# Program order for GpSimd and the SP queue in the first MLP product of a streaming encoder step

## The chip, the cores and the metric

The kernel runs on one core of one Trainium2 chip. The metric is the device time of one execution in microseconds (us); the times given are medians of several runs. The engines are named as the profile names them: PE is TensorE (PEld its weight loads), DVE is VectorE, ACT is ScalarE, POOL is GpSimd, and SP is SyncE, which here only issues DMAs. SP's queue works in order: while one DMA waits for its semaphore, those behind it wait too.

## The reference, cut to what matters

The reference is one inference step of a two-layer encoder over 1024 prompt tokens and 64 sample tokens, in fp32. Each layer ends with an MLP, the part that the change touches:

```
x = x + sq_relu_mlp(rmsnorm(x, norm_mlp[layer]), w_up[layer], w_down[layer])
def sq_relu_mlp(h, w_up, w_down):
    return jnp.square(jax.nn.relu(h @ w_up)) @ w_down
```

D_MODEL is 1024, D_FF 4096. The rest (pooling mixer and RG-LRU in layer 0, windowed attention in layer 1, cross-attention in both, norms, state outputs) is the same in both kernels.

## The kernel before, in words

Activations are kept transposed, features on the 128 partitions, tokens along the free axis. The 1088 tokens are cut into s = 0 (512 tokens) and s = 1 (576 tokens, worked on as two blocks of 288). Every fp32 product is made of three fp32r products of high and low parts, so each weight tile is loaded (`st`, line 174, three buffers), and split by ACT and DVE into `wp` (lines 186 and 187, three buffers). Class `Weights` does that along one plan of all weights: `ahead()` (line 192) splits up to two tiles beyond the one in use and loads as many further tiles as there are staging buffers.

The second product of the MLP, `mlp_down`, is one Strassen-like step with seven products (`SEVEN`). It needs sums of quarters of u (the squared activations) and sums of quarters of w_down. Both are made by POOL during the first product, `mlp_up` (line 934), and go through DRAM: u into `us`, the sums of weights into `sums`.

`mlp_up` loops over 16 turns q of two blocks f of 128 features. A turn works on one tile `u` (two buffers). For each f and each of three token blocks, `unit` multiplies (line 216, 24 matmuls), evacuates with the factor `rb` of the norm (DVE, line 969, into `t`, two buffers) and squares into u (ACT, lines 972 and 974). After both f, POOL makes four differences of u (line 990), and u is queued to be stored. Then `weights_sums(q)` loads quarters of w_down by two DMAs into the single buffer `quarters` (line 943) and POOL makes four sums (lines 947 to 950), queued to be stored too. `store()` (line 955) empties that one list, `todo`, after f = 0 of the next turn. In q = 0 and q = 15 the order of the blocks differs, so that s = 0 is used first; in q = 15, after s = 0's last block, four loads `load_u` (line 928) into `ur` (three buffers) and their splits `uhl` (lines 233 and 236) prepare the second product. `uhl` lies in the pool `hp`, whose eight buffers the two norms' pairs `hpH` and `hpL` fill until then.

`rb` comes from `Norm.columns` and `Norm.rows`: sums of squares `ss` (DVE, line 300), PE (line 310), `rc` (DVE, line 315), a power on POOL (line 316), transposes on PE (line 326), a copy on ACT (line 327). For s = 1 this is `prepared(1, G_MLP + l)`, called in line 1456 right before `mlp_up`.

What sets the order: the program states the instructions in an order, and a scheduler of the framework chooses the order of each engine's queue from it, by dependencies, priority and a simulation of its own. It may take `weights_sums` of later turns, which depend on nothing but their buffer, ahead of differences of u. A region `manual_schedule(engines=...)` makes the named engines issue the region's instructions in the stated order; other engines, and where instructions from outside the region fall among those inside, stay the scheduler's.

Of the kernel before, what the change touches and what calls it, by code (L numbers as in the profile page):

```python
# [24 lines left out]
G_MIX, G_CROSS, G_MEM, G_MLP, G_FIN = 0, 2, 4, 6, 8  # L25
# [21 lines left out]
def body(ctx, tc, I, O):  # L47
# [24 lines left out]
    def mm_bank():  # L72
        return bank(ps_mm, "mm")

    def s_bank():
        return bank(ps_s, "s")
# [54 lines left out]
    sums = [[scr.tile([128, 4, 2, 512], F32, name=f"sums{l}_{g}") for g in range(8)] for l in range(2)]  # L131
# [802 lines left out]
    def mlp_up(l, norms, p, outer):  # L934
        blocks = [(0, 0, 512), (1, 0, 288), (1, 288, 288)]
        us = [scr.tile([128, 7, 2, TH], F32, name=f"u{l}_{g}") for g in range(8)]
        todo, first = [], []

        def weights_sums(q):

            a = p.tile([128, 4, 512], F32, tag="quarters", name="quarters", bufs=1)
            for i in range(2):
                nc.sync.dma_start(a[:, 2 * i:2 * i + 2],
                                  I["w_down"][l][256 * q + 128 * i:256 * q + 128 * i + 128]
                                  .rearrange("p (h n) -> p h n", h=2))

            pool.tensor_tensor(a[:, 3], a[:, 1], a[:, 3], OP.add)
            pool.tensor_tensor(a[:, 1], a[:, 0], a[:, 1], OP.subtract)
            pool.tensor_tensor(a[:, 0], a[:, 3], a[:, 0], OP.subtract)
            pool.tensor_tensor(a[:, 2], a[:, 2], a[:, 0], OP.subtract)  # L950
            todo.append((sums[l][q // 2][:, :, q % 2], a))

        def store():
            while todo:
                nc.sync.dma_start(*todo.pop(0))

        for q in range(16):
            u = p.tile([128, 8, TH], F32, tag="u", name="u", bufs=2)
            wts = {}

            def unit(f, bi):
                s, b0, bn = blocks[bi]
                nm = norms[s]
                ps = s_bank() if q == 0 and s else mm_bank()
                dense(ps[:, :bn], wts[f], 0, KC, nm.pair.rhs(b0, bn))
                if q == 0 and f == 0 and b0 == 0:
                    nm.rows()
                t = p.tile([128, 512], F32, tag="t", name="t", bufs=2)
                dve.scalar_tensor_tensor(t[:, :bn], ps[:, :bn], 0.0, nm.rb[:, b0:b0 + bn], OP.max, OP.mult)  # L969
                slots = u[:, U21:U22 + 1] if f else u[:, U11:U12 + 1:U12 - U11]  # L970
                if s == 0:
                    act.activation(slots[:, :, :256], t.rearrange("p (a b) -> p a b", a=2), AF.Square)  # L972
                else:
                    act.activation(slots[:, b0 // 288, 256:], t[:, :bn], AF.Square)  # L974

            order = [[(f, bi) for bi in range(3)] for f in range(2)]
            if q in (0, 15):
                order = [[(0, 0)], [(1, 0), (0, 1), (0, 2), (1, 1), (1, 2)]]
            for f in range(2):
                wts[f] = W.get((("up", l), 2 * q + f))  # L980
                for o in order[f]:
                    unit(*o)
                    if q == 15 and o == (1, 0):
                        store()
                        first = [load_u(us, outer, 0, g) for g in range(4)]
                W.ahead()
                if f == 0:
                    store()
            for to, a, b in ((T1, U12, U11), (T3, U22, U12), (T2, U22, T1), (T4, T2, U21)):
                pool.tensor_tensor(u[:, to], u[:, a], u[:, b], OP.subtract)  # L990
            todo.append((us[q // 2][:, :, q % 2], u[:, :7]))
            weights_sums(q)
        store()
        return us, first

    def mlp_down(l, us, first, last, p, outer):
# [55 lines left out]
    class Window:  # L1052
# [124 lines left out]
        def store(self, ps, nm):  # L1177
            p = self.p
            nat = p.tile([128, 256], F32, tag="nat", name="nat", bufs=1)
            act.activation(nat, ps[:, :256], AF.Copy)  # L1180
            pool.dma_start(O[nm + "_p"][0, 0].rearrange("m k d -> m (k d)"), nat)
            nat = p.tile([128, 256], F32, tag="nat", name="nat", bufs=1)
            act.activation(nat[:64], ps[:64, 256:512], AF.Copy)
            pool.dma_start(O[nm + "_s"][0, 0, 64:128].rearrange("m k d -> m (k d)"), nat[:64])
# [182 lines left out]
    def prepared(s, g):  # L1367
        norm = Norm(s, g)
        for c in range(KC):
            norm.chunk(c)  # L1370
        norm.rows()
        return norm

    def phase(name):
        return tc.tile_pool(name=name, bufs=1, reuse_waits="tile")
# [24 lines left out]
    def main():  # L1400
        with phase("memory") as p:
            mem = memory_load(p)
            kv = memory_kv(p, *mem)
            next(kv)
            load_vectors(p)
            todo = [load_x(s) for s in range(2)]
            for _ in kv:
                for _ in range(5):
                    if todo and next(todo[0], "end") == "end":
                        todo.pop(0)  # L1410
            assert not todo
        norm = prepared(0, G_MIX)
        with phase("mixer") as p:
            q = Queue()
            mx = Mixer(p, q)
            first = mx.project(0, norm)
            for _ in IN_ORDER[1:]:
                next(first)
                q.step(5)
            next(first)  # L1420
            norm = prepared(1, G_MIX)
            q.step(5)
            second = mx.project(1, norm)
            for _ in range(3):
                next(second)
                q.step(5)
            while any(not job.done for job in mx.jobs[0]):
                q.step()
            project_back(0, ("out", 0), mx.y[0], q)
            mx.open[1] = True  # L1430
            for _ in second:
                q.step(5)
            c1 = prepared(0, G_CROSS)
            q.drain()
            project_back(1, ("out", 1), mx.y[1], order=[(0, 1, 2, 4, 5, 6), (7,), (3,)], spare=2)
            mx.states()
        for l in range(2):
            if l == 1:
                with phase("window") as p:
                    win = Window(p)  # L1440
                    win.caches()
                    win.project(0, norms[0])
                    win.attend()
                    norm = prepared(1, G_MIX + 1)
                    project_back(0, ("wo", 0), win.o, order=HALVES, spare=4)
                    win.project(1, norm)
                    win.attend()
                    c1 = prepared(0, G_CROSS + 1)
                    project_back(1, ("wo", 1), win.o, order=HALVES, spare=2)
            with phase(f"cross{l}") as p:  # L1450
                nexts = []
                cross(l, 0, c1, p, lambda: nexts.append(prepared(1, G_CROSS + l)))
                cross(l, 1, nexts[0], p, lambda: nexts.append(prepared(0, G_MLP + l)))
            with phase(f"mlp{l}") as outer:
                with phase(f"up{l}") as p:
                    up = mlp_up(l, [nexts[1], prepared(1, G_MLP + l)], p, outer)
                norms = [None, None]

                def last(s):
                    if s > l:  # L1460
                        while True:
                            yield
                    norms[s] = Norm(s, G_FIN, pair=False) if l else Norm(s, G_MIX + 1)
                    for c in range(4, 8):
                        norms[s].chunk(c)
                    for c in range(4):
                        yield
                        norms[s].chunk(c)
                    if l:
                        store_y(norms[s], s_bank)  # L1470
                    else:
                        norms[s].rows(s_bank)

                with phase(f"down{l}") as p:
                    mlp_down(l, *up, last, p, outer)

    main()


# [28 lines left out]
```

## Time and profile before

| | |
|---|---|
| Median of 3 runs | 2814.31 us (2809.4 to 2815.35) |
| Profiled execution, its own time | 2806.5 us |
| Its span, first to last instruction | 2804.7 us |
| Mean granted TensorE clock | 0.985 |
| Busy: PE, DVE, ACT, POOL | 2720.7, 1414.6, 1094.2, 535.8 us |

The span is what the instructions of the profiled execution cover; its own time is 1.8 us longer, and the median of the runs is 7.8 us above that execution. In the rows below times are us from the span's start. The first product of layer 0 begins at about 670 us and ends at about 1075 us; that of layer 1 lies at about 2040 to 2442 us. "x8" at a row's end counts merged instructions; "[9.93 <-POOL rc L316]" says that the engine sat idle for 9.93 us before it and what ended that.

### The profile page before, as it was taken

The page shows a single profiled execution, that of the slowest core. Times are in us where ns is not written, and L with a number is a line of the kernel's source. Part 1 is how long each engine was busy: PE and PEld are TensorE (multiplying, and loading weights), DVE is VectorE, ACT ScalarE, POOL GpSimd, SP SyncE. Part 2 cuts the span into 40 slices and gives each one's busy share as a digit, 9 for nine tenths or more (in the row PEclk, how much of TensorE's full clock was granted, in tenths as well). Part 3 has the DMA queues.
Part 4 walks back from the last instruction along what each step waited for, and adds up shares of the span by engine and source line. Part 5 has one row for each costly group of instructions (what it writes and reads, how often), then busy time and mean ns, then how long its engine had stood idle before and what let it go on. Part 6 is the DMA issues. An engine that isn't in the chain of part 4 may idle for free. (4 is left out here: it accounts for less than half of the span.)

```text
span 2804.7 us, 44507 instructions
## 1 busy us (share of the span) xinstructions
PE 2720.7 (97%) x18280; PEld 2540.8 (91%) x18280; DVE 1414.6 (50%) x2328; ACT 1094.2 (39%) x1929; POOL 535.8 (19%) x486
## 2 busy tenths in 40 slices
PE   8999999998998999999999999999989999999998
PEld 7978998897998999999988899989979989899998
DVE  5596766564322226455457558566532222464453
ACT  5584555352212124333337347344422112343334
POOL 3200000013455321000003013001245442300000
PEclk9999999999999999999999999999989999999999
DMA  8722232325666537555421321233366763465552
GB/s 269 226 83 75 68 102 81 106 84 173 221 224 222 181 129 242 186 186 178 132 66 31 86 71 38 88 92 99 113 203 209 253 232 127 142 238 182 176 179 79
DMA packets 364367, 411.89 MB, mean 147 GB/s; under 512 B 45840, under 2 KB 267040, under 8 KB 364164
## 3 DMA queue, kind: packets, MB, share of 16 engines
q1 hardware_dynamic: 355268, 382.00, 42.0%
q0 software_dynamic: 8896, 27.06, 2.9%
q8 instruction: 143, 2.34, 0.3%
q14 instruction: 60, 0.49, 0.1%
HBM read 299.74 MB, written 109.39 MB: 146 GB/s over the span
## 5 line engine op out<-in xcount | busy, mean ns | idle before, releaser
L216 PE MATMUL mm<-hpH,wp 128*128 128x288 f32 (+2 forms) x5952 | 1428.3, 329 | 16.9 <-DVE t L969 13.1
L216 PEld LDWEIGHTS mm<-hpH,wp 128*128 128x128 f32 x5952 | 1018.8, 189 | 98.4 <-DVE t L969 15.2
L216 PE MATMUL mm<-hpL,wp 128*128 128x288 f32 (+2 forms) x2976 | 932.9, 330 | 2.2 <-DVE hpL L291 2.2
L216 PEld LDWEIGHTS mm<-hpL,wp 128*128 128x128 f32 x2976 | 565.2, 190 | 42.0 <-DVE hpL L291 3.3
L186 ACT ACTIVATE wp<-st 128x1024 fp32r<-128x1024 f32 x282 | 297.8, 1058 | 672.3 <-PE mm L216 414.2
L187 DVE TENSOR_TENSOR wp<-st,wp 128x1024 fp32r<-128x1024 f32 x282 | 357.0, 1267 | 277.2 <-ACT wp L186 274.8
L969 DVE SCALAR_TENSOR_TENSOR t<-mm,rb 128x288 f32<-128x288 f32 (+1 forms) x184 | 99.1, 539 | 521.4 <-PE mm L216 458.0
L990 POOL TENSOR_TENSOR u<-u 128x544 f32<-128x544 f32 x128 | 203.8, 1606 | 233.3 <-ACT u L974 230.8
L316 POOL TENSOR_TENSOR rc<-rc,mhalf 128x4 f32<-128x4 f32 (+1 forms) x21 | 21.5, 1030 | 888.1 <-DVE rc L315 888.1
L972 ACT ACTIVATE u<-t 128x512 f32<-128x512 f32 x64 | 40.4, 632 | 371.2 <-DVE t L969 216.6
L1039 PE MATMUL s<-uhl,wd 128*128 128x256 f32 x560 | 156.5, 280 | 0.0
L1038 PE MATMUL s<-uhl,wd 128*128 128x256 f32 x560 | 156.1, 279 | 0.0
L1040 PE MATMUL s<-uhl,wd 128*128 128x256 f32 x560 | 156.0, 279 | 0.0
L236 DVE TENSOR_TENSOR uhl<-ur,uhl 128x1088 fp32r<-128x1088 f32 x112 | 146.2, 1307 | 16.5 <-ACT uhl L233 16.4
L186 ACT ACTIVATE wd<-st 128x1024 fp32r<-128x1024 f32 x70 | 73.9, 1056 | 199.5 <-PE t L1040 157.0
L216 PE MATMUL s<-hpH,wp 128*128 128x288 f32 (+1 forms) x576 | 141.4, 330 | 0.0
L233 ACT ACTIVATE uhl<-ur 128x1088 fp32r<-128x1088 f32 x112 | 123.1, 1103 | 36.6 <-DMA ur<-u 32.4
L216 PEld LDWEIGHTS s<-hpH,wp 128*128 128x128 f32 x576 | 98.1, 188 | 8.0 <-ACT hpH L233 0.3
L1038 PEld LDWEIGHTS s<-uhl,wd 128*128 128x128 f32 x560 | 105.3, 188 | 0.0
L1039 PEld LDWEIGHTS s<-uhl,wd 128*128 128x128 f32 x560 | 105.1, 188 | 0.0
L1040 PEld LDWEIGHTS s<-uhl,wd 128*128 128x128 f32 x560 | 105.0, 187 | 0.0
L187 DVE TENSOR_TENSOR wd<-st,wd 128x1024 fp32r<-128x1024 f32 x70 | 87.8, 1254 | 32.4 <-ACT wd L186 32.2
(367 smaller groups left out, 4798.7 us busy)
## 6 DMA issues: line engine op xcount, KB each, us to landing
u<-u SPq DMA_DIRECT2D x32, 1904.0 KB, 8.4
ur<-u SPq DMA_DIRECT2D x112, 544.0 KB, 5.7
quarters<-in_w_down_dram SPq DMA_DIRECT2D x64, 512.0 KB, 5.2
sums<-quarters SPq DMA_DIRECT2D x32, 1024.0 KB, 5.4
st<-in_w_up_dram SPq DMA_DIRECT2D x64, 512.0 KB, 6.6
st<-sums SPq DMA_DIRECT2D x64, 512.0 KB, 5.5
st<-in_w_down_dram SPq DMA_DIRECT2D x48, 512.0 KB, 4.7
st<-in_w_mq_dram SPq DMA_DIRECT2D x32, 512.0 KB, 3.6
```

Source lines behind the costliest of these rows:

```text
L186: act.activation(wt[:, 0], st, AF.Copy)
L187: dve.tensor_tensor(wt[:, 1], st, f32(wt[:, 0]), OP.subtract)
L216: pe.matmul(ps, a, b, start=i == 0, stop=i == len(terms) - 1)
L233: act.activation(h, src, AF.Copy)
L236: dve.tensor_tensor(l, src, f32(h), OP.subtract)
L316: pool.tensor_tensor(rc[:m, b0:b1], rc[:m, b0:b1], mhalf[:m, b0:b1], OP.pow)
L969: dve.scalar_tensor_tensor(t[:, :bn], ps[:, :bn], 0.0, nm.rb[:, b0:b0 + bn], OP.max, OP.mult)
L972: act.activation(slots[:, :, :256], t.rearrange("p (a b) -> p a b", a=2), AF.Square)
L990: pool.tensor_tensor(u[:, to], u[:, a], u[:, b], OP.subtract)
L1038: pe.matmul(ps, wl, uh, start=first, stop=False)
L1039: pe.matmul(ps, wh, ul, start=False, stop=False)
L1040: pe.matmul(ps, wh, uh, start=False, stop=half == 1 and g == 3 and k == 1)
```

## The change

The list of stores is split in two, `todo` for sums of u and `kept` for sums of weights. After f = 0 of a turn only the store of u is issued; the weights' store is issued after f = 1, just before the turn's own differences of u are stated. Everything in `mlp_up` that runs on SP and POOL is put into a region in which these two engines keep the stated order. `prepared(1, ...)` is called ahead of that region.

```diff
-        todo, first = [], []
+        todo, kept, first = [], [], []
...
-            todo.append((sums[l][q // 2][:, :, q % 2], a))
-
-        def store():
+            kept.append((sums[l][q // 2][:, :, q % 2], a))
+
+        def store(todo):
             while todo:
                 nc.sync.dma_start(*todo.pop(0))
...
                 for o in order[f]:
                     unit(*o)
                     if q == 15 and o == (1, 0):
-                        store()
+                        store(todo)
+                        store(kept)
                         first = [load_u(us, outer, 0, g) for g in range(4)]
                 W.ahead()
                 if f == 0:
-                    store()
+                    store(todo)
+            store(kept)
             for to, a, b in ((T1, U12, U11), (T3, U22, U12), (T2, U22, T1), (T4, T2, U21)):
                 pool.tensor_tensor(u[:, to], u[:, a], u[:, b], OP.subtract)
             todo.append((us[q // 2][:, :, q % 2], u[:, :7]))
             weights_sums(q)
-        store()
+        store(todo)
+        store(kept)
         return us, first
...
-                    up = mlp_up(l, [nexts[1], prepared(1, G_MLP + l)], p, outer)
+                    own = [nexts[1], prepared(1, G_MLP + l)]
+                    with tc.manual_schedule(engines={mybir.EngineType.SP, mybir.EngineType.Pool}):
+                        up = mlp_up(l, own, p, outer)
```

## Rows read from the trace of the kernel before

**Rows 1.** Waits of PE, whole span: total us, times, longest us.

```profile
PE t L326 <- POOL rc L316: 21.8, 6, 9.9
PE mm L216 <- DVE t L969: 13.1, 5, 4.5
...
PE t L310 <- DVE ss L300: 4.7, 2, 2.7
PE s L1038 <- DVE wp L187: 4.4, 2, 2.2
```

**Rows 2.** Busy time by stretch: busy us (count) of each engine, PEclk, DMA share, GB/s.

```profile
667.00:690.00 23.00, 10.34 (x56) 8.34 (x54) 11.74 (x14) 7.39 (x11) 11.52 (x10) 0.78 0.46 139
...
940.00:963.60 23.60, 23.60 (x147) 21.71 (x146) 5.67 (x8) 4.93 (x8) 6.81 (x5) 1.00 0.38 128
```

**Rows 3.** Waits of ACT from 700 to 930 us: total, times, longest.

```profile
ACT u L972 <- DMA u<-u: 79.8, 6, 19.1
```

**Rows 4.** Groups from 714 to 927 us: busy, mean ns, idle before, releaser.

```profile
L990 POOL TENSOR_TENSOR u<-u 128x544 f32<-128x544 f32 x36 | 52.7, 1481 | 5.8 <-ACT u L974 5.1
...
L947 POOL TENSOR_TENSOR quarters<-quarters 128x512 f32<-128x512 f32 x11 | 16.2, 1472 | 98.8 <-DMA quarters<-in_w_down_dram 98.8
```

**Rows 5.** Timeline of DVE, the 512-column evacuations: start us, us, instruction.

```profile
714.71 0.69 DVE L969 SCALAR_TENSOR_TENSOR t<-mm,rb 128x512 f32<-128x512 f32 x1 [3.14 <-PE mm L216]
...
927.32 0.69 DVE L969 SCALAR_TENSOR_TENSOR t<-mm,rb 128x512 f32<-128x512 f32 x1 [1.81 <-PE mm L216]
...
1033.58 0.69 DVE L969 SCALAR_TENSOR_TENSOR t<-mm,rb 128x512 f32<-128x512 f32 x1 [3.08 <-PE mm L216]
...
2085.81 0.69 DVE L969 SCALAR_TENSOR_TENSOR t<-mm,rb 128x512 f32<-128x512 f32 x1 [3.14 <-PE mm L216]
...
2294.68 0.69 DVE L969 SCALAR_TENSOR_TENSOR t<-mm,rb 128x512 f32<-128x512 f32 x1 [3.13 <-PE mm L216]
```

**Rows 6.** Timeline at the start of the product, both layers.

```profile
667.82 3.70 DVE L291 SCALAR_TENSOR_TENSOR hpL<-x,gcol,hpH 128x576 fp32r<-128x576 f32 x2 [1.53 <-PE mm L216]
...
671.80 5.13 DVE L291 SCALAR_TENSOR_TENSOR hpL<-x,gcol,hpH 128x576 fp32r<-128x576 f32 x6
...
678.95 0.22 DVE L315 TENSOR_SCALAR rc<-t 128x4 f32<-128x4 f32 x2 [0.75 <-PE t L310]
...
688.92 1.53 POOL L316 TENSOR_TENSOR rc<-rc,mhalf 128x4 f32<-128x4 f32 x2
...
2050.73 0.22 DVE L315 TENSOR_SCALAR rc<-t 128x4 f32<-128x4 f32 x2 [1.63 <-PE t L310]
...
2060.14 1.12 PE L326 MATMUL t<-ident,rc 128*128 128x128 f32 x4 [7.45 <-POOL rc L316]
```

**Rows 7.** Timeline of an undisturbed turn of layer 0: PE, POOL and SP.

```profile
957.33 0.39 PE L216 MATMUL mm<-hpL,wp 128*128 128x512 f32 x1
...
958.81 4.84 POOL L990 TENSOR_TENSOR u<-u 128x544 f32<-128x544 f32 x3 [9.79 <-ACT u L974]
...
963.67 0.52 SPq L955 DMA_DIRECT2D u<-u  x1
```

**Rows 8.** The page's DMA issues: count, KB each, median us to landing.

```profile
u<-u SPq DMA_DIRECT2D x32, 1904.0 KB, 8.4
ur<-u SPq DMA_DIRECT2D x112, 544.0 KB, 5.7
```

**Rows 9.** DMAs of the tile quarters, loads and stores.

```profile
DMA to landing us min/median/max: 3.5/5.3/10.3
```

**Rows 10.** Timeline at the turn to the second product of layer 0.

```profile
1061.48 8.81 SPq L928 DMA_DIRECT2D ur<-u  x4
...
1070.22 1.21 DVE L187 TENSOR_TENSOR wp<-st,wp 128x1024 fp32r<-128x1024 f32 x1
...
1079.52 2.35 DVE L187 TENSOR_TENSOR wp<-st,wp 128x1024 fp32r<-128x1024 f32 x1
...
1090.81 1.06 ACT L186 ACTIVATE wd<-st 128x1024 fp32r<-128x1024 f32 x1 [12.18 <-DMA u<-u]
```

## The prediction

> **What bounds the kernel now.** I first read the busy line of the page and the waits of TensorE: it works 97% of the span, so the change can only give back time in which it waits or runs at the lower clock, or add such time. The four waits that lie in or beside the two MLP stages [rows 1] are 21.8 us behind POOL's rc (nearly all of it one wait of 9.9 us and one of 7.45 us, one per layer), 13.1 us behind DVE's t (five waits), 4.7 us behind ss and 4.4 us behind a weight split. Next come the stretches of the first layer [rows 2]: in an undisturbed stretch of 23.6 us TensorE is busy throughout at clock 1.00, while around the start of the product it works 10.34 us of 23 at clock 0.78.
>
> What stands behind the 13.1 us? ScalarE's square, which writes u, waited six times, 79.8 us in all, for the store of an earlier u to land [rows 3]. u has two buffers; ScalarE stops, then DVE (t has two buffers as well), then the two mm banks are full and TensorE stops. The store is late because of POOL's order. Between 714 and 927 us POOL runs 11 sets of weight sums and waits 98.8 us for their quarters [rows 4], against 9 turns of q (36 differences, four each): the scheduler runs the weights ahead of u. A set takes load, sums and store in a row through the single quarters buffer, and every difference behind it waits along.
>
> What it costs is read from the pace, by t's 512-column evacuations, one per f. Undisturbed, nine steps from 927.32 to 1033.58 take 106.26 us: 11.81 us each, 23.6 us a turn. The seventeen steps from 714.71 to 927.32 should take 200.7 us; they took 212.6 us, and the same seventeen in layer 1, from 2085.81 to 2294.68, took 208.9 us [rows 5]. So **11.9 and 8.2 us** are lost, the idle time and the lower clock after it together.
>
> The 9.9 us is the same order once more, at the start. rc's input is ready from 678.95 us on, but the power (first of two at 688.92, 1.53 us both) stands on POOL behind a set of weight sums that waits for its DMA; in layer 1 rc is ready at 2050.73 and the transposes start at 2060.14 [rows 6].
>
> **The change part by part.** *POOL in program order.* A turn then issues four differences of u, and then its own set of weight sums (two loads, four additions, one store): one set to one turn. No difference can stand behind a weight set of a later turn. The power of rc is emitted before the region; the region's first POOL instruction, the first difference of q = 0, needs blocks that have been multiplied by rb, which is made from that rc. So POOL has to run the power first, and three to four sets per layer that ran ahead of the product move behind it.
>
> *Start, layer 0.* The power could start at about 679.1 rather than 688.92: the wait of 9.9 us shrinks to about 0.2 us (TensorE's own last matmuls before it): 9.7 us. Beside those weight sums two of DVE's norm splits took 3.70 us; six without them took 5.13 us, 0.86 each [rows 6]. That is 2.0 us of a DVE chain that has no idle time up to ss, for which TensorE waits 2.7 us: 2.0 us. Together **11.7 us**. *Layer 1:* the 7.45 us go (TensorE has work until past 2052), and of the 2.0 us behind ss I take 1.9, by the same reading: **9.3 us**. Of the clock at the start I take no gain. The rows bound it: if it does not fall, some 2 us more in layer 0 and 3 in layer 1; if it falls as long as before with the engine now working, some 2 to 3 us less in each.
>
> *The loop.* Count from a turn's first matmul S = 957.33 [rows 7]. The last three differences of the turn before start at 958.81, take 4.84 us, and the u store goes at 963.67, S + 6.3. It lands 8.4 us later by its median [rows 8], at about S + 15; the buffer is wanted again from about S + 29 (next turn plus the first block). Cover: 14 us. So the u waits go: **11.9 + 8.2 us**. On SP the u store stands behind one load of w_up and in front of the next, which may go only about S + 14; so its wait for POOL holds nothing up. The weights store comes after that load, at about S + 14.5, lands by the median of its tile, 5.3 us [rows 9], at S + 20, and only then may the next quarters load go, with a w_up load behind it that isn't due before the next turn's S + 2. Three staged tiles cover a delay there. The weight sums of a turn run from about S + 6.5 to S + 12 of the next one (four of some 1.3 us), before their store's place. These moves I cost at nothing; the cover is u's 14 us.
>
> *The turn to the second product.* Here something is lost. Three of the four first loads of u (ur) went out long before; the fourth only at 1061.48 [rows 10]. In program order all four stand in the last turn behind the store of weights 14, which has to wait for POOL: S + 12 of that turn, about 1064. They take 5.7 us to land [rows 8], so the first three splits start at about 1070, and the fourth, which waits for a ur buffer, is ready at about 1081. TensorE wants the first at 1075 and is held up there today by a split that starts at 1079.52 and takes 2.35 us (an undisturbed one at 1070.22 took 1.21) [rows 10]. On ScalarE and DVE late u splits can hold squares and weight splits behind them. Bounds: today's 2.2 us per layer gone, or the fourth split's lateness passed on whole, 8 us. I take **3 us lost per layer**, nearer to the low end since g = 0 to 2 come in time and give TensorE 8 us of work. Behind the product the last set of weights now follows the differences: SP's last store waits some 5 us longer, with loads of w_down behind it. That is hidden by the first half of the step, some 20 us: ScalarE there waits for the u store anyway, until 1090.81 [rows 10].
>
> The Trainium skill (SBUF — State Buffer, section "SBUF: two separate sides") says that GpSimd and VectorE share one port pair, held for a whole instruction, so that the other is blocked. The traces agree: 2.35 us against 1.21 us for the same split beside POOL. By that rule the last set of weight sums, now just behind the differences, would slow two or three more weight splits by 1.1 us each, an estimate of 2 to 3 us per layer at this very place; by the rows alone, where those splits have time left, nothing.
>
> **Sum.** 11.7 + 9.3 + 11.9 + 8.2 = 41 us gained, 6 lost: 35 us. The profiled execution took 2806.5 us, which makes 2771; the median of the three runs shown is 2814.3, 7.8 us above it, which makes **2779 us**.
>
> **The rivals.** (a) *The late ur loads cost the full 8 us, with a drop of the clock of 2 us, in each layer.* For it: the fourth split was waited for even when the three others came early. Against: the work that g = 0 to 2 give. 41 less 20 is 21 us: 2793 us. (b) *More than I count:* the short waits at start and turn vanish wholly and the clock stays up: 41 + 4 + 5 is 50 us: 2764 us. (c) *The change does not do what it says:* the region fixes order within itself alone; if the scheduler still places other SP or POOL work so that u or rc waits as before, 2814 us. Against it: rc's power cannot come behind the region. (d) *Slower: the ring of weight sums becomes the bound.* Load, sums, store through one buffer must now fit into each turn of 23.6 us, since SP and POOL may not pass it by. Today the 11 sets take about 19 us each, 213 us over 11 [rows 4]. Every microsecond over 23.6 costs 32 us (16 turns, 2 layers); it decides from 24.7 us on, where 35 us are eaten. With both DMAs at their longest, 10.3 us each [rows 9], and four sums at the 1.47 us of L947 [rows 4], it is 26.5 us: 2.9 x 32 is 93, less 35 makes it 58 us slower, 2872 us. Against it: the medians, and that DMA has more room when the weights are spread over the whole product.
>
> **How the numbers follow.** Forecast 0.64, (a) 0.18, (b) 0.08, (c) 0.04, (d) 0.06. Predicted 2779 us. From 2764 to 2800 the range holds the forecast's own uncertainty (clock, turn), (a) and (b); (c) and (d) stay out. A measurement of this kernel tells about 0.2%, 5.6 us, from no change. Faster by more: 0.90; within: 0.04; slower: 0.06.
>
> **What would show it.** Right: no wait of ScalarE's square for a u store; TensorE's wait for rc below 1 us in both MLP stages; weight sums strictly one set per turn; steps of 11.8 us without a gap from the second turn to the last. Wrong: a turn longer than 23.6 us, POOL or SP waiting for quarters with u behind them, or waits of TensorE over 5 us at the first matmuls of the second product.

## The result, and the profile after

The changed kernel takes 2771.35 us, the median of four runs (2769.47 to 2772.14), against 2812.9 us of four runs of the kernel before on the same chip: a ratio of 0.9852, 95% interval 0.9835 to 0.9869. That is 41.5 us less; the forecast was 2779 us, 35 us less, and its range 2764 to 2800 us holds the result. The profiled execution took 2772.14 us, its span 2770.3 us, at a mean granted clock of 0.991; PE is busy for 2712.8 us of it, 98%.

The waits of PE over the whole span (total us, times, longest us), against [rows 1]:

```profile
PE t L326 <- POOL rc L316: 7.0, 6, 3.2
...
PE s L1041 <- DVE wp L187: 4.9, 2, 2.5
PE s L1041 <- DVE wd L187: 4.6, 3, 3.1
```

The wait for rc has lost 14.8 us, the waits for t (13.1 us) and ss (4.7 us) are gone. The wait for the split of wp at the turn to the second product is still there, 2.5 us a layer where it was 2.2. One line is new, waits for splits of wd, 3.1 us at the longest. They make 4.6 of the 7.7 us that the ends lose in the table below.

The start of the product, by stretch (us, busy us and count of PE, PEld, DVE, ACT, POOL, then PEclk, DMA share, GB/s). The first row is the same stretch of time as in [rows 2], the second lies around the wait for rc:

```profile
667.00:690.00 23.00, 21.80 (x129) 18.99 (x128) 11.91 (x18) 9.44 (x15) 2.51 (x2) 1.00 0.16 47
675.00:695.00 20.00, 18.80 (x115) 16.52 (x114) 7.51 (x13) 5.87 (x10) 2.89 (x3) 1.00 0.09 27
```

PE works 21.80 us of 23 where it worked 10.34, and its clock stays at 1.00 where it was 0.78. The timeline of the start, against [rows 6]:

```profile
671.23 1.55 DVE L291 SCALAR_TENSOR_TENSOR hpL<-x,gcol,hpH 128x576 fp32r<-128x576 f32 x2 [1.75 <-PE mm L216]
673.06 4.46 DVE L291 SCALAR_TENSOR_TENSOR hpL<-x,gcol,hpH 128x576 fp32r<-128x576 f32 x6
...
679.68 1.21 DVE L187 TENSOR_TENSOR wp<-st,wp 128x1024 fp32r<-128x1024 f32 x1
...
679.78 2.51 POOL L316 TENSOR_TENSOR rc<-rc,mhalf 128x4 f32<-128x4 f32 x2 [52.61 <-DVE rc L315]
...
681.83 0.65 PE L326 MATMUL t<-ident,rc 128*128 128x128 f32 x4 [1.20 <-POOL rc L316]
...
2030.38 2.51 POOL L316 TENSOR_TENSOR rc<-rc,mhalf 128x4 f32<-128x4 f32 x2 [52.60 <-DVE rc L315]
```

POOL starts the power as soon as DVE has made its input. It had been idle for over 52 us: no set of weights runs ahead of the product any more. DVE's eight norm splits take 1.55 + 4.46 us in place of 3.70 + 5.13.

In the loop, ScalarE's wait for a u store (79.8 us, [rows 3]) is gone; from 700 to 930 us its two longest lines are now

```profile
ACT u L972 <- DVE t L969: 91.6, 19, 4.9
ACT u L974 <- DVE t L969: 43.6, 19, 2.4
```

which is the pace of PE: nothing behind it holds it up. t's 512-column evacuations, first and last of an even stretch in each layer, against [rows 5]:

```profile
704.97 0.69 DVE L969 SCALAR_TENSOR_TENSOR t<-mm,rb 128x512 f32<-128x512 f32 x1 [3.14 <-PE mm L216]
...
1035.55 0.69 DVE L969 SCALAR_TENSOR_TENSOR t<-mm,rb 128x512 f32<-128x512 f32 x1 [3.08 <-PE mm L216]
...
2055.59 0.69 DVE L969 SCALAR_TENSOR_TENSOR t<-mm,rb 128x512 f32<-128x512 f32 x1 [3.14 <-PE mm L216]
...
2386.18 0.69 DVE L969 SCALAR_TENSOR_TENSOR t<-mm,rb 128x512 f32<-128x512 f32 x1 [3.08 <-PE mm L216]
```

28 steps lie between the two of each layer, 330.6 us: 11.81 us a step in both, the undisturbed pace of before. One turn on POOL and SP, against [rows 4, 7]:

```profile
724.65 4.84 POOL L992 TENSOR_TENSOR u<-u 128x544 f32<-128x544 f32 x3 [9.73 <-ACT u L974]
729.44 1.29 POOL L947 TENSOR_TENSOR quarters<-quarters 128x512 f32<-128x512 f32 x1
...
729.51 0.53 SPq L955 DMA_DIRECT2D u<-u  x1
...
737.83 0.53 SPq L955 DMA_DIRECT2D sums<-quarters  x1
744.09 0.82 SPq L943 DMA_DIRECT2D quarters<-in_w_down_dram  x2
```

Differences, then one set of weight sums, which finds its quarters loaded; the store of u goes out behind the differences, the next quarters are loaded behind the store of the sums.

The turn of layer 0, against [rows 10]: SP, ScalarE, PE and one split of DVE, and then, by stretch, the time of the second wait.

```profile
1042.42 9.10 SPq L928 DMA_DIRECT2D ur<-u  x4
...
1057.74 1.21 DVE L187 TENSOR_TENSOR wp<-st,wp 128x1024 fp32r<-128x1024 f32 x1
...
1059.01 0.39 PE L1041 MATMUL s<-uhl,wp 128*128 128x256 f32 x1 [2.48 <-DVE wp L187]
...
1062.94 0.52 SPq L955 DMA_DIRECT2D u<-u  x1
1070.09 0.52 SPq L955 DMA_DIRECT2D sums<-quarters  x1
1070.66 2.85 SPq L928 DMA_DIRECT2D ur<-u  x3
1073.56 6.02 SPq L174 DMA_DIRECT2D st<-in_w_down_dram  x3
...
1075.73 2.01 ACT L186 ACTIVATE wd<-st 128x1024 fp32r<-128x1024 f32 x2 [11.35 <-DMA sums<-quarters]
...
1085.08 0.39 PE L1041 MATMUL s<-uhl,wd 128*128 128x256 f32 x1 [3.13 <-DVE wd L187]
```

```profile
1083.00:1092.00 9.00, 6.92 (x44) 6.66 (x45) 7.62 (x9) 5.33 (x6) 0.00 (x0) 0.81 0.79 267
```

Between the store of the last u (1062.94) and that of the last sums (1070.09) SP issues nothing: it waits for POOL's last set. Six loads of ur and st stand behind it. The second half of the step gets its weights late, PE waits 3.13 us, and the clock falls to 0.81 around that. The first wait has changed its cause: before, the split of wp that PE waits for took 2.35 us beside POOL's differences [rows 10], now it takes 1.21 us and PE waits for it all the same.

All kernels can be laid side by side by stretches of their own traces. **Start** is from a layer's first 512-column evacuation to that of q = 1, **loop** from there to that of q = 15, **end** from there to the last matmul of the second product (us):

| kernel | start 0 | loop 0 | end 0 | start 1 | loop 1 | end 1 |
|---|---|---|---|---|---|---|
| before | 37.2 | 342.5 | 360.6 | 37.4 | 338.8 | 361.7 |
| after | 26.9 | 330.6 | 364.5 | 26.9 | 330.6 | 365.4 |

In the kernel before, the first of these evacuations itself came late, 2.6 us behind its matmuls in layer 0 and 1.9 in layer 1, held up with DVE's norm splits; that lies ahead of "start" in the table, and with it the starts give 12.9 and 12.4 us. (The ends of matmuls are modelled; counted from the first 512-column matmul, the starts give 13.1 and 12.6 us.) Together: 12.9 + 12.4 + 11.9 + 8.2 gained, 3.9 + 3.8 lost at the ends, 37.7 us. The two spans differ by 34.4 us, because the stages ahead of the first MLP, with PE's order the same, took some 3 us more in the profile after. From one profile to the next the first layer's first evacuation stood anywhere from 673 to 681 us; so the experiments are read by these stretches first, and by ratios second.

The ends have a scatter of their own. The end of layer 1 took 361.7 us in the kernel before, and 363.2 us in experiments 1 and 5 below, whose turn has the same wait of PE, 2.2 us. What differs is TensorE's granted clock in the 8 us behind that wait (1.00 and 0.79, the column PEclk); first the kernel before, then experiment 1, layer 1:

```profile
2449.10:2457.10 8.00, 7.81 (x62) 7.82 (x63) 2.43 (x2) 0.00 (x0) 1.34 (x1) 1.00 0.69 238
```

```profile
2453.80:2461.80 8.00, 7.76 (x50) 7.76 (x51) 2.48 (x2) 0.00 (x0) 1.39 (x1) 0.79 0.69 236
```

So about 1.5 of the 3.8 us lost at the end of layer 1 is the clock of that one profile, and a difference of 1 or 2 us between single ends shows little.

### The profile page after: what moved, and what is told of

Its sections match the earlier page's. It is cut to its first block, busy times and chain, and to the rows that moved or that the text cites. A ratio compares the mean times of both kernels' runs of the same rounds, so it can differ in the third digit from the quotient of the medians.

```text
span 2770.3 us, 44519 instructions
## 1 busy us (share of the span) xinstructions
PE 2712.8 (98%) x18280; PEld 2535.7 (92%) x18280; DVE 1393.6 (50%) x2328; ACT 1096.1 (40%) x1929; POOL 541.5 (20%) x486
## 5 line engine op out<-in xcount | busy, mean ns | idle before, releaser
L216 PEld LDWEIGHTS mm<-hpL,wp 128*128 128x128 f32 x2976 | 562.3, 189 | 41.5 <-DVE hpL L291 3.1
L187 DVE TENSOR_TENSOR wp<-st,wp 128x1024 fp32r<-128x1024 f32 x282 | 344.8, 1224 | 271.3 <-ACT wp L186 266.7
L992 POOL TENSOR_TENSOR u<-u 128x544 f32<-128x544 f32 x128 | 218.6, 1718 | 382.5 <-ACT u L974 380.0
L974 ACT ACTIVATE u<-t 128x288 f32<-128x288 f32 x128 | 55.9, 436 | 144.0 <-DVE t L969 144.0
```

The costliest lines, as they stand in the source:

```text
L187: dve.tensor_tensor(wt[:, 1], st, f32(wt[:, 0]), OP.subtract)
L216: pe.matmul(ps, a, b, start=i == 0, stop=i == len(terms) - 1)
```

## The experiments

### 1 and 2: the names alone, the region alone

Experiment 1 is the changed kernel without its region, experiment 2 the kernel before with the region and its one list of stores.

```diff
 # experiment 1
-                    with tc.manual_schedule(engines={mybir.EngineType.SP, mybir.EngineType.Pool}):
-                        up = mlp_up(l, own, p, outer)
+                    up = mlp_up(l, own, p, outer)
 # experiment 2, against the kernel before
-                    up = mlp_up(l, [nexts[1], prepared(1, G_MLP + l)], p, outer)
+                    own = [nexts[1], prepared(1, G_MLP + l)]
+                    with tc.manual_schedule(engines={mybir.EngineType.SP, mybir.EngineType.Pool}):
+                        up = mlp_up(l, own, p, outer)
```

> Only the two lists of stores, no region. Theory (the region does it, since it keeps weight sums of later turns from running ahead of u and of rc's power): the scheduler still lets the weights run ahead, ratio to the kernel before 0.998 to 1.004, TensorE's wait for rc 9 us and 7 us, ScalarE's waits for the u store some 70 us in the first layer. Rival (naming the u store ahead of the weights' store is what frees u): the waits for the u store go, some 20 us faster, ratio 0.993, with the rc wait left.

> The region with the old single list: the weights' store stands right behind the u store after f = 0. Theory: the same as the changed kernel within 0.2% (ratio to before 0.983 to 0.988), no waits for rc over 1.5 us, no waits for the u store; the new place of the weights' store is worth nothing, since u's store has 14 us to spare. Rival (the order of the two stores matters): SP waits for POOL's weight sums with w_up loads behind, TensorE waits in the loop, 10 us or more slower than the changed kernel, ratio above 0.989.

Experiment 1: 2808.18 us, ratio 0.9997 (0.9984 to 1.0009). Start 37.5 and 37.8 us, loop 342.6 and 339.9. Its waits of ScalarE from 700 to 930 us are those of before:

```profile
ACT u L972 <- DMA u<-u: 79.8, 6, 18.9
```

Experiment 2: 2767.24 us, ratio 0.9852 (0.9829 to 0.9875), start 26.9, loop 330.6, end 363.4 and 365.5 us. The region is the whole of the change; which store is stated first is worth nothing that can be measured, with it or without it.

### 3 and 4: POOL alone, SP alone

```diff
-                    with tc.manual_schedule(engines={mybir.EngineType.SP, mybir.EngineType.Pool}):
+                    with tc.manual_schedule(engines={mybir.EngineType.Pool}):    # experiment 4: SP
```

> The changed kernel with program order kept on POOL alone; SP's queue is ordered by the planner again. Theory (POOL's order is what frees rc and the tiles u; SP's order brings nothing and costs at the turn, because the last weights' store stands ahead of loads there): the start of a layer's first product takes 26.9 us as in the changed kernel (before: 37.2 and 37.4), its loop 330.6 us (before: 342.5 and 338.8), and the stretch from the turn to the product's end falls from 364 to 365 us to between 360 and 362 us; the whole is 3 to 10 us faster than the changed kernel, ratio to before 0.982 to 0.984. Rival (SP's order is needed as well: the planner lets loads of weights run ahead and POOL follows its own order with stores of u behind them): waits of ScalarE for u come back, the loop is over 335 us, and the ratio is over 0.989.

> The changed kernel with program order kept on SP's queue alone; POOL is ordered by the planner again. Theory (POOL's order is what frees rc and u): the start goes back to 36 to 38 us, the loop to 338 to 343 us, ratio to before 0.995 to 1.000. Rival (the one load of quarters per turn that SP's order leaves already holds POOL to one set per turn, so POOL has nothing to run ahead with): start 26.9 us and loop 330.6 us, within 3 us of the changed kernel.

POOL alone: 2768.02 us, 0.985 (0.983 to 0.987). SP alone: 2768.09 us, 0.9852 (0.9833 to 0.987). Both have start 26.9 and loop 330.6 us in both layers: either order alone is enough, so in 4 the rival was right and my theory, that POOL's own order is needed, fell. The tile `quarters` shows how, SP alone in the first fence, POOL alone in the second (duration ns, first and last start us, up to the turn of layer 0):

```profile
L943 SPq DMA_DIRECT2D quarters<-in_w_down_dram x32: 340/414/1697, 693.2 to 1051.1; - x32
```

```profile
L943 SPq DMA_DIRECT2D quarters<-in_w_down_dram x32: 328/383/428, 631.2 to 1052.4; - x32
L947 POOL TENSOR_TENSOR quarters<-quarters x16: 1282/1289/2267, 708.7 to 1067.8; 128x512 f32<-128x512 f32 x16
```

In the kernel before, these loads went from 624.8 to 893.7 us. With SP in order they are spread over the product, and POOL has nothing to run ahead with; with POOL in order the first set's quarters come as early as before, and its sums wait until 708.7 all the same. The other half of my expectation of 3 fell too: with the loads of ur back in earlier turns, the ends are 364.2 and 366.8 us, no better than in the changed kernel, and PE's first wait there is longer, 4.3 us.

### 5: order kept over the first turn only

```diff
         for q in range(16):
+            with ExitStack() as only:
+                if q == 0:
+                    only.enter_context(tc.manual_schedule(engines={mybir.EngineType.SP, mybir.EngineType.Pool}))
...
```

> The region covers the first turn only; from the second on the scheduler may let weights run ahead again. It separates the start from the loop. Theory: the start gains as in the changed kernel (rc waits of some 1 us, about 12.5 us per layer), while the loop falls behind again (ScalarE waits for u stores, at least as long as before, as more sets are left to run ahead in the loop: loop loss 10 to 30 us per layer). Time between the two kernels or near the kernel before: ratio 0.990 to 1.005. Rival (the start's order alone makes the gain, the loop's stalls followed from it): ratio 0.986.

2784.96 us, ratio 0.9912 (0.9891 to 0.9933). Start 26.9 us in both layers; loop 341.9 and 342.5, end 360.6 and 363.2, with ScalarE's wait back (700 to 930 us):

```profile
ACT u L975 <- DMA u<-u: 53.5, 4, 16.4
```

The gains of start and loop are separate: an order kept at the start doesn't help the turns that follow, and the loop loses 8 to 12 us a layer wherever the weights may run ahead.

### 6 and 7: what the turn costs, two guesses that fell

Experiment 6 puts the first four loads of ur ahead of the stores that wait for POOL. Experiment 7 takes `quarters` from the pool of the whole MLP, so that no `wd` of the second product lies on its bytes and ScalarE's wait at 1075.73 for the store of the sums can't be.

```diff
 # experiment 6
-                        store(todo)
-                        store(kept)
                         first = [load_u(us, outer, 0, g) for g in range(4)]
+                        store(kept)
 # experiment 7
-            a = p.tile([128, 4, 512], F32, tag="quarters", name="quarters", bufs=1)
+            a = outer.tile([128, 4, 512], F32, tag="quarters", name="quarters", bufs=1)
```

> The changed kernel with the first four loads of ur of the second product placed ahead of the stores at the turn in program order, so that they are not behind the store of weight sums that SP holds at 1041.9 us. Theory (the late first loads of ur are what the turn costs): PE's first wait at the turn, 2.5 us, goes, and the stretch from the turn to the product's end falls by 2 to 4 us per layer, whole 4 to 8 us faster than the changed kernel, ratio 0.982 to 0.984. Rival (SP is held by the last weights' store, to about 1070 us, and the loads of the step's second half are behind it): the second wait stays and the whole is within 2 us of the changed kernel.

> The changed kernel with the tile of quarters in the pool that lives through both products, so that no weight tile of the second product lies on its bytes. Theory (the new waits at the turn to the second product, 3.1 us in layer 0 and 1.2 us in layer 1 behind a weight split, come from ScalarE's wait for the last store of weight sums, 11.4 us): that wait becomes one for the u store or goes, TensorE's second wait falls below 0.5 us, 3 to 7 us faster than the changed kernel in all. Rival (the late loads of u are what costs at the turn): TensorE's waits there stay as they are, within 1.5 us of the changed kernel.

Experiment 6: 2768.29 us, 0.9859 (0.9835 to 0.9883); the first wait shrinks to 1.9 and 1.5 us, but later ones take its place, and the ends are 362.9 and 368.2 us, 731.1 together against 730.0 after. Late first loads of ur are not, by themselves, what the turn costs; SP's last store still held up the later loads here. Experiment 7: 2771.93 us, 0.9869 (0.9845 to 0.9892), ends 364.4 and 367.3 us. ScalarE's wait for the sums is gone, the loss is not. Its trace shows what holds the step now, SP's queue and then ScalarE:

```profile
1072.05 0.52 SPq L955 DMA_DIRECT2D sums<-quarters  x1
1072.62 0.62 SPq L928 DMA_DIRECT2D ur<-u  x1
...
1076.14 0.53 SPq L928 DMA_DIRECT2D ur<-u  x1
...
1079.03 1.11 ACT L233 ACTIVATE uhl<-ur 128x1088 fp32r<-128x1088 f32 x1 [5.40 <-DMA ur<-u]
```

ScalarE waits for ur, and ur's load stood behind the last sums' store. From here the theory is that SP, held by that store, costs the turn.

### 8 and 9: the weight sums in the middle of a turn

Both state a turn's weight sums after f = 0, so that the last set comes ahead of the last differences. They differ in which store stands first, and in whether a store stands ahead of the first loads of ur.

```diff
                 if f == 0:
-                    store(todo)
-            store(kept)
+                    store(todo)          # experiment 9: store(kept), then store(todo)
+                    store(kept)
+                    if q:
+                        weights_sums(q)
...
-            weights_sums(q)
-        store(todo)
-        store(kept)
+            if not q:
+                weights_sums(q)
+        store(kept)
+        store(todo)
```

> The changed kernel with each turn's weight sums named in the middle of the turn, behind the store of the differences of the turn before, in place of the end of it, so that the last set of weight sums is done before the last differences of u and no load is behind its store. Theory (SP held by the last weights' store costs the turn's second wait): the second wait of PE at the turn (3.1 and 1.2 us) goes, the stretch from the turn to the product's end falls by 2 to 4 us per layer, start and loop stay within 1 us of the changed kernel's, whole 3 to 8 us faster. Rival (POOL in the middle of a turn makes the differences of u late): ScalarE waits for u in the loop and the loop grows by 3 us or more; or the turn stays as it is, and the whole is within 2 us of the changed kernel.

> As the weight sums in the middle of the turn, but with the store of a set of weight sums placed ahead of the store of the differences of u, and nothing ahead of the first four loads of ur. Theory (that kernel's loop was held by a ring: load of quarters 5 us, set 5.4, differences 5.4 to 6.4, stores, and 9 us until the next load of quarters, together 26.3 us against the turn's 23.6): without the differences in the ring it is some 20 us, the loop is back at 330.6 us, and as the last set is done before the last differences, the stretch from the turn to the product's end falls from 364 to 365 us to between 360 and 362 us; whole 2762 to 2768 us, ratio 0.982 to 0.985. Rival (the middle of the turn is the wrong place whatever the order): loop over 333 us, ratio over 0.99.

Experiment 8: 2868.91 us, ratio 1.0216 (1.0196 to 1.0236), loop 342.8 and 346.7 us, ends 401.6 and 401.2. This is rival (d) of the prediction, come about by another edit: a ring through the one buffer `quarters`, with the differences in it. One lap on POOL and SP:

```profile
874.58 0.82 SPq L943 DMA_DIRECT2D quarters<-in_w_down_dram  x2
...
879.62 1.30 POOL L947 TENSOR_TENSOR quarters<-quarters 128x512 f32<-128x512 f32 x1 [16.11 <-DMA quarters<-in_w_down_dram]
...
884.98 6.43 POOL L994 TENSOR_TENSOR u<-u 128x544 f32<-128x544 f32 x4
...
891.44 0.53 SPq L955 DMA_DIRECT2D u<-u  x1
892.07 0.61 SPq L955 DMA_DIRECT2D sums<-quarters  x1
900.89 0.82 SPq L943 DMA_DIRECT2D quarters<-in_w_down_dram  x2
```

From load to load it is 26.3 us, where a turn has 23.6: 5.0 until the quarters are there, 5.4 for the sums, 6.5 for the differences, 0.6 for the store of u, 8.8 from the store of the sums to the next load. The lag is felt once the cover of u's second buffer is used up, from about 870 us on: ScalarE waits for u 17 times in the two layers, 230.0 us, and the loops lose 12.2 and 16.1 us. The ends lose 37.1 and 35.8 us more, since there the first loads of ur stand behind the store of the last sums and PE waits up to 38.8 us. Experiment 9 takes the differences out of the ring (the sums' store no longer stands behind that of u): 2768.6 us, 0.9857 (0.9843 to 0.9872), start 26.9 and loop 330.6 us. So the ring is shown. The turn did not gain: ends 364.8 and 367.1 us. The last sums ran beside DVE's splits and pushed the last differences back, and u's last store went at 1063.37, 30.6 us behind q = 15's first evacuation, where the changed kernel has 27.4.

### 10: the last store on another queue

`quarters` as in experiment 7, and the last set's store issued by POOL's queue, so that SP goes on to the loads.

```diff
         store(todo)
-        store(kept)
+        while kept:
+            nc.gpsimd.dma_start(*kept.pop(0))
         return us, first
```

> The changed kernel with the last set's store issued by POOL's queue in place of SP's, and the tile of quarters in the space of the whole MLP, so that no tile of the second product lies on its bytes. Theory (SP, held by the last store until about 1070 us, is what makes the loads of the step's second half late): PE's second wait at the turn (3.1 and 1.2 us) goes and the stretch from the turn to the product's end falls by 2 to 4 us per layer, whole 4 to 8 us below the changed kernel, ratio 0.982 to 0.984. Rival (the last differences and their store, which come at 1063 us in any case, set when the second half can begin): stretch still 364 to 367 us, whole within 2 us of the changed kernel.

2761.01 us (2760.07 to 2765.05), ratio 0.9829 (0.9815 to 0.9844). The ends are 361.4 and 364.0 us, 4.6 us less in all than in the changed kernel, 6.4 and 6.6 less than in experiments 7 and 9. The timeline in layer 0 (PE, SP, POOL, DVE):

```profile
1058.80 0.38 PE L1042 MATMUL s<-uhl,wp 128*128 128x256 f32 x1 [2.53 <-DVE wp L187]
...
1062.73 0.52 SPq L955 DMA_DIRECT2D u<-u  x1
1063.30 7.43 SPq L928 DMA_DIRECT2D ur<-u  x3
...
1064.03 2.23 POOL L948 TENSOR_TENSOR quarters<-quarters 128x512 f32<-128x512 f32 x1
...
1065.03 2.31 DVE L187 TENSOR_TENSOR wd<-st,wd 128x1024 fp32r<-128x1024 f32 x1
...
1082.67 0.39 PE L1042 MATMUL s<-uhl,wd 128*128 128x256 f32 x1 [0.97 <-DVE wd L187]
```

The loads of ur go right behind u's store, at 1063.30 where they went at 1070.66, and the second wait of PE falls from 3.13 to 0.97 us; in layer 1 it falls from 1.24 to 0.3. The first wait stays, and the clock behind it is that of the changed kernel in both layers (1.00 in layer 0, about 0.8 over 8 us in layer 1), so the scatter of the clock there does not make the difference. The theory holds for the larger part: SP, held by the last weights' store, is 4.6 of the 7.7 us that the ends had lost. The second wait alone doesn't measure this cost. In experiment 2 SP is held for the same 7.1 us, and the second wait of layer 0 is 0.27 us: there PE came late already, after a first wait of 2.76 us and 12 us at a clock of 0.72. (The store on POOL's queue was not tried with `quarters` in its old place.) This is the fastest version here: experiments 9 and 11, run beside it on the same chip, took 2768.6 and 2772.9 us. Against the changed kernel itself the gain stands in the stretches; the two ratios' intervals overlap.

### 11 and 12: the last turn left free, all sums stored by POOL

```diff
 # experiment 11: as experiment 5, with
-                if q == 0:
+                if q < 15:
 # experiment 12: as experiment 7, with
-            kept.append((sums[l][q // 2][:, :, q % 2], a))
+            nc.gpsimd.dma_start(sums[l][q // 2][:, :, q % 2], a)
```

> Program order kept over the first fifteen turns of q alone; the planner orders POOL and SP in the last turn, as in the kernel before: it puts the last set of weight sums ahead of the last differences and loads three tiles ur during earlier turns. Theory (the turn's loss comes from the order of the last turn): start 26.9 us, loop 330.6 us, and the stretch from the turn to the product's end 360 to 362 us as in the kernel before; whole 4 to 8 us below the changed kernel, ratio 0.982 to 0.984. Rival (the turn's loss belongs to the faster loop, whose last differences come with less slack, whatever the order): stretch 364 to 367 us, whole within 2 us of the changed kernel.

> As with the last set's store on POOL's queue, but with the store of every set of weight sums issued by POOL, right behind its set, so that SP is held by none of them and the first loads of ur of the second product go out at about 1037 us in place of 1042.4. Theory (what holds SP at the turn is what PE waits for there): PE's first wait at the turn falls from 2.5 to under 2 us, no second wait comes back, start 26.9 us and loop 330.6 us as before, the stretch from the turn to the product's end 360 to 361.5 us in the first layer; whole 2757 to 2761 us, ratio 0.981 to 0.983. Rival (PE's first wait is set by the splits that DVE and ScalarE have to do in those microseconds, not by when ur comes): the first wait stays at 2 us or more and the whole is within 2 us of the kernel with the last store alone on POOL; or the issue on POOL, 0.75 us each, makes the differences of u late, and the loop grows.

Experiment 11: 2772.9 us, 0.9869 (0.9853 to 0.9886), ends 365.5 and 371.6 us. This is not the last turn of the kernel before, where the last set of sums was stored by 909.2 us: here the scheduler puts that set between the first and the other three differences, from 1050.11 to 1058.16 us. The split of wp that PE waits for takes 2.28 us beside it, and PE's first wait is 5.4 us in both layers. Experiment 12: 2770.56 us, 0.986 (0.9843 to 0.9878), loop 330.6, ends 364.3 and 367.2 us. Here SP is free and six loads of ur go at once, and PE's first wait grows all the same. SP, DVE, PE:

```profile
1036.51 16.54 SPq L928 DMA_DIRECT2D ur<-u  x6
...
1058.09 1.29 DVE L236 TENSOR_TENSOR uhl<-ur,uhl 128x1088 fp32r<-128x1088 f32 x1
1059.30 1.22 DVE L187 TENSOR_TENSOR wp<-st,wp 128x1024 fp32r<-128x1024 f32 x1
...
1060.57 0.39 PE L1041 MATMUL s<-uhl,wp 128*128 128x256 f32 x1 [3.49 <-DVE wp L187]
```

The split of wp for which PE waits stands on DVE behind splits of u that are not needed yet. Experiments 3, 6, 11 and 12 all bring ur earlier, and none makes the two ends together cheaper. By these timelines the first wait follows the order of the splits on ScalarE and DVE; that is a reading, and an order of them that would remove the wait was not tried.

## Why the prediction was right, and where it was not

**The mechanism, right.** Weight sums ahead of u cost the loop, and ahead of rc the start; with one set per turn both go. Experiment 5 separates the two, experiment 1 shows that the names have no part in it.

**The loop, 11.9 + 8.2 us: exact.** All steps are 11.81 us, and loop 0 is 11.9 and loop 1 8.2 us shorter.

**The start, 11.7 and 9.3 us: too small, 12.9 and 12.4 measured.** The wait for rc fell to 1.2 us a layer, not to the 0.2 forecast, and so missed the sign "below 1 us": the power itself took 2.51 us for the 1.53 of [rows 6]. The wait for ss went wholly, 2.7 and 2.0 us, as DVE's eight norm splits, now without sums beside them, gained 2.8 us in layer 0, not the 2.0 counted. (The six that I took as undisturbed were not all so: in the kernel before, POOL's last sum of that set ran from 670.98 to 672.67 us, beside the first of them. Undisturbed, one takes 0.74 us, not 0.86.) The waits make 8.7 + 2.7 in layer 0 and 6.25 + 2.0 in layer 1; what is left, 1.5 and 4.1 us, is the clock, of which I took nothing and gave bounds of 2 and 3 us, the second too low. It was 0.66 and 0.57 over the 20 us around rc in the kernel before, and is 1.00 after.

**The turn, 3 us a layer: 3.9 and 3.8, but by another way.** The step that failed is that SP's last store is "hidden by the first half of the step, some 20 us". It was not: that is the second wait of PE, which experiment 10 takes away. The step that I priced, the late first loads of ur, shows little of its own: the first wait went from 2.2 to 2.5 us, and experiment 6, with those loads early, gained nothing. (With SP free as well, in experiment 12, the first wait grew; what those loads cost in the best order stays open.) And 1.5 of the 3.8 us is the clock of one profile. So the size was nearly right by chance, and the reason mostly wrong.

By the Trainium skill (SBUF — State Buffer, section "SBUF: two separate sides") I gave the last set of weight sums another price, 2 to 3 us a layer, since GpSimd and VectorE would block each other there. They do: in experiment 10 the split of wd beside the last sums takes 2.31 us, against 1.2 alone. But these slower splits are there with the second wait of PE mostly gone, so they lie beside other work, and the rows' price of nothing for this point was the better one for this order. In experiment 11, where the set runs beside the split that PE waits for, it is not nothing.

**The rivals.** (a), the full 8 us a layer at the turn, did not come. (b), clock up and waits gone, came at the start only, and there but for 1.2 us a layer. (c) is ruled out by the loop. (d), the ring of `quarters`, did not come in the changed kernel, where the sums and the differences are not in one ring; experiment 8 shows the mechanism, at 26.3 us a lap. Its price there was 28 us in the loops, where my working, 32 us for each microsecond over 23.6, would make it 86: u's buffer covers the first turns of each layer. (That its time is near the 2872 us of that rival is chance, as its ends cost more than its loops.)

**The sum** by stretches is 37.7 us against 35; the medians, 41.5 us apart (36.8 to 46.4 by the ratio's interval), agree with the sum of 37.7, and the forecast of 35 lies just below that interval. The base that I took, the median of three runs at 2814.3 us, stands 1.4 us above that of the four runs compared here.

## What to carry to other kernels

Where a scheduler may let cheap background work with its own buffer run ahead, look for the engine queue on which it gets ahead of work that others wait for; one queue kept in program order was enough here, whether that of the engine or that of the loads which feed it. Then look at the last turn, where the background work has no following turn to hide in: its last store belongs on a queue on which no load is due. And before a step is moved within a turn, add up the lap of the buffer that it goes through, with everything that the new order puts in between, and compare it with the turn.

## What was not expected of the hardware

POOL's two powers of rc take 2.51 us in both layers with a split of DVE beside them (679.68, 1.21 us), and took 1.53 us where DVE was idle; the split keeps its 1.21 us. Here only POOL waits; beside its last sums in experiment 10 both do (2.23 us for the 1.29 of 729.44, and 2.31 for 1.2). By the Trainium skill (SBUF — State Buffer, section "SBUF: two separate sides") the one that starts first holds the shared ports; the split did start 0.1 us ahead of the power.

TensorE's clock behind a short wait is not told by the wait's length here. Waits of 1.20 us at the start, 2.22 (kernel before, layer 1), 2.48 (changed kernel, layer 0) and 2.53 us (experiment 10, layer 0) left it at 1.00, its upper level. Waits of 2.22 (kernel before, layer 0), 2.41 (changed kernel, layer 1) and 2.38 us (experiment 10, layer 1) went with 0.79 over 8 us around or behind them. No run shows what decides.

A store issued by POOL costs POOL 0.73 to 0.75 us of its own time, sixteen times a layer in experiment 12, without slowing the loop (330.6 us).
